# Where the weights lie in a partition: moving the weight buffers below the accumulator and the normalised input in a two-layer recurrent trunk

## The chip, the core and the metric

The kernel runs on one core of one Trainium2 chip. The metric is the device time of one execution in microseconds; the kernel before has a median of 2709.31 us over 3 runs (2709.21 to 2709.97). A profile is one further execution, recorded instruction by instruction.

## What is computed

The reference is a decoder trunk of two layers over 512 positions of 2048 channels, everything in float32:

```
for layer in range(2):
    x = x + mixer(rmsnorm(x) @ w_in) @ w_out
return rmsnorm(x, final_norm)
```

The mixer of layer 0 splits the columns of its projection into an RG-LRU group, an mLSTM group (4 heads) and a gate. The mixer of layer 1 is a Mamba-2 SSD mixer in 8 groups. Nearly all the arithmetic lies in the projections: 128 x 128 blocks of weights against 512 positions.

## The kernel before

**Layout of the work.** Channels lie on the 128 partitions, positions along the free axis. The residual stream `acc` is 16 tiles of [128, 512]. A projection of one column tile is 16 contraction tiles, and a product of two float32 numbers is made of three passes in the type float32r: each weight is split into a rounded part and a rest (`whi`, `wlo`), each moving operand likewise (`xh`/`xl` for the normalised input, `yh`/`yl` and their relatives for what goes into the output projections). The three matmuls are lines 138 to 140:

```
pe.matmul(ps, wh, mh, start=first, stop=False)   # L138
pe.matmul(ps, wh, ml, start=False, stop=False)   # L139
pe.matmul(ps, wl, mh, start=False, stop=last)    # L140
```

"Weights" here is the stationary operand, which a LDWEIGHTS brings into the array ahead of each matmul; the "moving" operand streams past it, 512 columns at a time. So a projection of one column tile is 48 matmuls (a chain), and one group of an output projection is 12 per column tile.

**What is a weight and what moves.** Input projections (tiles `xm`, `zm`, `xl`, `zl` of layer 0, `dt`, `xbc`, `z` of layer 1) move `xh` and `xl`. Output projections (`po`) move `yh`/`yl`, `ylh`/`yll`, `ymh`/`yml`; the head's projections `v`, `o`, `qk` move `xmh`/`xml` or `xch`/`xcl`; one head's `po` moves `xh`/`xl`, which then hold its y. In the last stage the weights of the last output projection are held in `xh` and `xl` themselves. A few matmuls use `ones_r` as weights (`rs`, sums over partitions), and the attention's `num` uses `vh`/`vl` as weights and `Ph`/`Pl` as the moving operand.

**Loads.** `load_w` (line 116) issues one DMA of 512 KB into `wraw`, and per 512 columns ScalarE writes `whi` (line 131) and VectorE writes `wlo` (line 132), at a high priority. There are two `wraw`, four `whi` and four `wlo`, in rotation. The tile framework orders instructions by priority and inserts the waits.

**Staged work.** Everything else of the mixers (convolutions, gates, scans, attention) is in generators that go on after a number of weight chunks, so that TensorE always has a chain to run. Softplus of the LRU's decay, `nlam` (lines 339 and 340, with the helpers at lines 185 to 202), is done once, at the start, on VectorE in three small tiles `ln`.

**Memory.** SBUF pools are stacked: a pool opened later lies above those opened earlier, and a tile lies behind the one allocated before it in its pool, rounded up to 32 bytes. The program's first tile, `prm`, begins at byte 16,512 of each partition and has 3,488 bytes. Adding up the sizes gives the places before: `acc` from byte 22,624; `xh` 55,392 to 88,159; `xl` 88,160 to 120,927; `wraw` 125,088; `whi` 133,280 to 141,471; `wlo` 141,472 to 149,663; above that the pools of each layer, `y` of layer 0 from 182,752 and of layer 1 from 204,512.

Of the kernel before, what the change touches and what calls it, by code (L numbers as in the profile page):

```python
# [9 lines left out]
F32 = mybir.dt.float32  # L10
# [6 lines left out]
P = 128  # L17
# [6 lines left out]

# columns of the packed per-partition parameter array
_W = [
# [12 lines left out]
NPAR = _o  # L39
# how many weight chunks pass before each stage of the mixers' work  # L40
LAG = dict(P=6, rs=2, late=3, dtr=15, CB=5, xtr=6, st=4, yo=1, att_rs=4, vtr=2, aitr=12, num=7, pr=2)
# where the column tiles of the previous group's output projection go in
VB = (2, 2)
# [4 lines left out]
def trunk(ctx, tc, x_t, par, w_in0, w_qkvo, w_lru, w_if, w_out0, w_in1, w_out1, out):  # L48
# [4 lines left out]
    cst = ctx.enter_context(tc.tile_pool(name="cst", bufs=1))  # L53
    wp = ctx.enter_context(tc.tile_pool(name="wp", bufs=1))
    pmm = ctx.enter_context(tc.tile_pool(name="pmm", bufs=3, space=PSUM))
# [16 lines left out]
    v.memset(eps, EPS)  # L72
    warm = cst.tile([P, 1], F32, name="warm")
    sc.activation(warm, eps, AF.Square)
    ones_r = cst.tile([P, P], F32R, name="ones_r")
    ones = ones_r.bitcast(F32)
    r_bc = cst.tile([P, S], F32, name="r_bc")
    acc_t = cst.tile([P, KD, S], F32, name="acc")
    acc = [acc_t[:, k] for k in range(KD)]
    xh = [cst.tile([P, S], F32R, name=f"xh{k}") for k in range(KD)]  # L80
    xl = [cst.tile([P, S], F32R, name=f"xl{k}") for k in range(KD)]
    xpairs = list(zip(xh, xl))
    raws = [cst.tile([P, S + 3], F32, name=f"raw{i}") for i in range(2)]
    for t in raws:
# [6 lines left out]

# [1 line left out]
    gens = []  # L93
# [20 lines left out]

# [1 line left out]
    def load_w(src, dsts=(None, None), pieces=1, ahead=3000):  # L116
# [24 lines left out]

    # one chunk: four contraction tiles, from the k-th on, of n
    def chunk(ps, w, mov, k, n):
# [22 lines left out]

    # in pieces: a reciprocal is slow, and the weights' splits go in between
    def recip(dst, src, w=S):
        for o in range(0, w, P):
            v.reciprocal(dst[:, o:o + P], src[:, o:o + P])  # L170

    # dst = 1 / sqrt(ssq / n + eps) on all partitions; ssq: per-partition partial sums
    def rstd(dst, ssq, n):
# [9 lines left out]

    # log1p(e) for 0 <= e <= 1 as 2 atanh(e / (2 + e))
    def log1p(dst, e, t1, t2):
        v.tensor_scalar(t1, e, 2.0, None, op0=ADD)
        v.reciprocal(t1, t1)
        v.tensor_tensor(t1, e, t1, op=MUL)
        v.tensor_tensor(t2, t1, t1, op=MUL)
        v.tensor_scalar(dst, t2, 1.0 / 15, 1.0 / 13, op0=MUL, op1=ADD)  # L190
        for c in (11, 9, 7, 5, 3, 1):
            v.tensor_tensor(dst, dst, t2, op=MUL)
            v.tensor_scalar(dst, dst, 1.0 / c, None, op0=ADD)
        v.scalar_tensor_tensor(dst, t1, 2.0, dst, op0=MUL, op1=MUL)

    # softplus(s * x) for s = +-1
    def softplus(dst, x, s, t0, t1, t2):
        v.scalar_tensor_tensor(t0, x, -1.0, x, op0=MUL, op1=MAX)
        sc.activation(t0, t0, AF.Exp, scale=-1.0)
        log1p(dst, t0, t1, t2)  # L200
        v.tensor_scalar(t0, x, s, 0.0, op0=MUL, op1=MAX)
        v.tensor_tensor(dst, dst, t0, op=ADD)

    # out of PSUM, ahead of other work: the tensor engine needs the bank
    def evac(o, a, b, op):
        with tc.high_priority(offset=1000):
            v.tensor_tensor(o, a, b, op=op)  # L207

    # causal convolution of a padded tile (bias included)
    def conv(dst, raw, w, b):  # L210
# [3 lines left out]

    # the two parts of acc * norm
    def prenorm(k, norm):
# [9 lines left out]

    # acc += w_out[rows of group g].T @ y, some column tiles
    def outproj(w_out, g, ys, js, done=None):
# [9 lines left out]

    # ================= layer 0 =================
    qd = [dr.tile([2, P, S], F32, name=f"qd{h}") for h in range(NH)]  # L240
# [10 lines left out]

    nlam = L0.tile([P, 16], F32, name="nlam")
    aiT = L0.tile([P, 16], F32, name="aiT")
    ln = [L0.tile([P, 16], F32, name=f"ln{i}") for i in range(3)]

# [29 lines left out]

# [1 line left out]
    pA = tc.tile_pool(name="A", bufs=1)  # L287
# [6 lines left out]

    # four contraction tiles at a time, in the four column strips of the array
    def gate_mm(kt, rhs):
# [4 lines left out]

    # the first two column tiles go along with the loads of x
    ps01 = [mmt("xm"), mmt("xm")]
# [6 lines left out]
    for h in range(NH):  # L310
        xm, xc = [], []
        for t in range(4):
            j = 4 * h + t
            if j > 1:
                ps = mmt("xm")
                proj(ps, w_in0[16 + j], xpairs)
            else:
                ps = ps01[j]
            if j == 0:
                v.tensor_tensor(ssq0[0], ssq0[0], ssq0[1], op=ADD)  # L320
                spawn(rstd(r_bc, ssq0[0], D))
                drain()
            raw = next_raw()
            evac(raw[:, 3:], ps, r_bc, MUL)
            m = xslot("xm")
            split(m[0], m[1], raw[:, 3:])
            xm.append(m)
            a = st("ca")
            conv(a, raw, pc("cm_w", 4 * j, 4), pc("cm_b", j))
            s = st("cs")  # L330
            sc.activation(s, a, AF.Sigmoid)
            v.tensor_tensor(a, a, s, op=MUL)
            c = xslot("xc")
            split(c[0], c[1], a)
            xc.append(c)
            tick()
            if j == 0:
                # -8 softplus(-lam)
                softplus(nlam, pc("lam", 0, 16), -1.0, *ln)
                v.tensor_scalar(nlam, nlam, -8.0, None, op0=MUL)  # L340
# [64 lines left out]

    # gates of all heads: ai = i - G, M = max(0, cummax ai), exp(-m) = exp(-(G + M))
    ready = []

    def gates():
        g_s = st("gs")  # L410
        sc.copy(g_s, ps_g)
        yield 1
        pg = axt("pg")
        pe.matmul(pg[0:36], pc("gsel", 0, 36), g_s, start=True, stop=True)
        g_i, g_f, g_t0, g_t1, g_t2 = [st(f"g{i}")[0:4] for i in range(5)]
        g_G = st("gG")[0:4]
        v.tensor_scalar(g_i, pg[0:4], pc("b_i")[0:4], None, op0=ADD)
        sc.copy(g_f, pg[32:36])
        v.tensor_scalar(g_f, g_f, pc("b_f")[0:4], None, op0=ADD)
        softplus(g_G, g_f, -1.0, g_t0, g_t1, g_t2)  # L420
        for c in range(4):
            cs = slice(c * P, (c + 1) * P)
            v.tensor_tensor_scan(g_t0[:, cs], ones[0:4], g_G[:, cs],
                                 0.0 if c == 0 else g_t0[:, c * P - 1:c * P], op0=MUL, op1=ADD)
        # g_t0 = -G
        v.tensor_tensor(g_i, g_i, g_t0, op=ADD)
        v.tensor_tensor_scan(g_t1, g_i, g_i, 0.0, op0=MAX, op1=MAX)
        v.tensor_tensor(g_t2, g_t0, g_t1, op=SUB)
        sc.activation(g_t2, g_t2, AF.Exp)
        dma(md[0:NH], g_t1)  # L430
        dma(md[NH:2 * NH], g_t2)
        ready.append(True)
        yield LAG["aitr"]
        pt = axt("aitr")
        for s in range(4):
            pe.transpose(pt[:, 4 * s:4 * s + 4], g_i[:, s * P:(s + 1) * P], ident[0:4, 0:4])
        sc.copy(aiT, pt[:, 0:16])
        ready.append(True)

# [1 line left out]
    def lru_tile(j, out_y):  # L441
# [46 lines left out]

# [1 line left out]
    def attention(h, yl, out_y):  # L490
# [115 lines left out]

    # ================= layer 1 =================
    dad = dr.tile([64, S], F32, name="dad")
    ed = dr.tile([64, S], F32, name="ed")
    dcd = dr.tile([64, 2], F32, name="dcd")  # L610

# [1 line left out]
    ps = mmt("dt")  # L613
# [12 lines left out]
    dcb = lt("dcb", shape=(P, 64, 2))  # L626
    na = lt("na", shape=(P, 1))[0:64]
    dc = lt("dc", shape=(P, 2))[0:64]

# [29 lines left out]

    # input projection, convolution and silu of one channel tile of x | B | C  # L660
    def xbc(j, dst):
# [27 lines left out]
    def pair(G, t, xs):  # L689
# [33 lines left out]
        yield LAG["st"]  # L723
        # states at the chunk boundaries
        pst = axt("st")
# [5 lines left out]
        for c in (1, 2):  # L731
# [3 lines left out]
            v.tensor_tensor(Sx[:, c], Sx[:, c], pst[:, c * P:(c + 1) * P], op=ADD)  # L735
        # within the chunks
        pd = axt("yd")
# [5 lines left out]
        yield LAG["yo"]  # L743
        # from the states
        po = axt("yo")
# [75 lines left out]

# [1 line left out]
    wl = []  # L823
# [39 lines left out]

# column tiles, contraction chunks of 8 tiles, each [128, 8 * 128] and contiguous
def _wpack(w):
# [4 lines left out]

# pairs of column tiles, contraction chunks of 4 tiles
def _wpair(w):
# [73 lines left out]
```

## Time and profile before

| what | value |
|---|---|
| median of 3 runs | 2709.31 us |
| profiled execution, span | 2708.4 us |
| TensorE matmul busy | 2680.3 us, 12462 instructions |
| VectorE busy | 1729.7 us |
| ScalarE busy | 1191.2 us |
| GpSimd busy | 118.5 us |
| granted TensorE clock, mean | 0.997 |
| DMA | 297.74 MB, 34.1% of 16 engines' span |

How to read it: "busy" is the union of an engine's recorded intervals. Matmuls are pipelined, so that one is recorded as longer than the distance to the next: the distance from start to start (called the pace below) is what counts, and it is read from the timeline, whose first two columns are the start and the duration in us. In the groups by line, `out<-in` names first what is written, then the moving operand, then the weights.

### The profile page before, as it was taken

The page shows a single profiled execution, that of the slowest core. Times are in us where ns is not written, and L with a number is a line of the kernel's source. Part 1 is how long each engine was busy: PE and PEld are TensorE (multiplying, and loading weights), DVE is VectorE, ACT ScalarE, POOL GpSimd, SP SyncE. Part 2 cuts the span into 40 slices and gives each one's busy share as a digit, 9 for nine tenths or more (in the row PEclk, how much of TensorE's full clock was granted, in tenths as well). Part 3 has the DMA queues.
Part 4 walks back from the last instruction along what each step waited for, and adds up shares of the span by engine and source line. Part 5 has one row for each costly group of instructions (what it writes and reads, how often), then busy time and mean ns, then how long its engine had stood idle before and what let it go on. Part 6 is the DMA issues. An engine that isn't in the chain of part 4 may idle for free.

```text
span 2708.4 us, 33237 instructions
## 1 busy us (share of the span) xinstructions
PE 2680.3 (99%) x12462; PEld 2176.9 (80%) x12462; DVE 1729.7 (64%) x2940; ACT 1191.2 (44%) x1882; POOL 118.5 (4%) x116
## 2 busy tenths in 40 slices
PE   8999999999999999999999999999999999999997
PEld 6778778777888888888888888888888888888887
DVE  8453535387757657665786667656677566675666
ACT  6343333356436436453555343443434434344445
POOL 1000000000000000000200000000000000000004
PEclk9999999999999999999999999999999999999999
DMA  4334342433333333323243332323324233242332
GB/s 164 115 112 135 98 139 90 157 100 122 114 107 105 114 103 107 103 90 99 96 126 109 109 109 94 124 94 109 109 89 130 94 106 111 87 125 95 107 98 101
DMA packets 114385, 297.74 MB, mean 110 GB/s; under 512 B 11688, under 2 KB 34472, under 8 KB 114224
## 3 DMA queue, kind: packets, MB, share of 16 engines
q1 hardware_dynamic: 114224, 295.62, 34.1%
q8 instruction: 98, 1.61, 0.2%
q14 instruction: 63, 0.52, 0.1%
HBM read 278.52 MB, written 17.06 MB: 109 GB/s over the span
## 4 chain that ended last, share of the span: by engine, by line
PE 96%; DVE 3%; DMA 1%; issue 0%; ACT 0%; POOL 0%; SPq 0%; DVEq 0%; ACTq 0%; POOLq 0%
PE po L140 8%; PE po L139 8%; PE po L138 8%; PE xbc L138 7%; PE xbc L140 7%; PE xbc L139 7%; PE z L138 4%; PE z L139 4%; PE z L140 4%; PE xl L138 2%; PE xm L138 2%; PE xm L140 2%; PE xl L139 2%; PE zm L140 2%; PE zm L139 2%; PE xl L140 2%
## 5 line engine op out<-in xcount | busy, mean ns | idle before, releaser
L131 ACT CAST whi<-wraw 128x512 fp32r<-128x512 f32 x886 | 545.7, 616 | 1211.6 <-PE po L139 255.4
L132 DVE TENSOR_TENSOR wlo<-wraw,whi 128x512 fp32r<-128x512 f32 x886 | 609.9, 689 | 467.1 <-ACT whi L131 434.0
L138 PE MATMUL xbc<-xh,whi 128*128 128x512 f32 x768 | 306.8, 399 | 0.0
L139 PE MATMUL xbc<-xl,whi 128*128 128x512 f32 x768 | 303.6, 395 | 0.0
L140 PE MATMUL xbc<-xh,wlo 128*128 128x512 f32 x768 | 303.6, 395 | 0.0
L207 DVE TENSOR_TENSOR acc<-acc,po 128x512 f32<-128x512 f32 (+1 forms) x272 | 176.5, 651 | 172.4 <-PE po L140 171.8
L138 PE MATMUL z<-xh,whi 128*128 128x512 f32 x512 | 205.0, 400 | 0.0
L139 PE MATMUL z<-xl,whi 128*128 128x512 f32 x512 | 202.4, 395 | 0.0
L140 PE MATMUL z<-xh,wlo 128*128 128x512 f32 x512 | 202.3, 395 | 0.0
L138 PE MATMUL po<-yh,whi 128*128 128x512 f32 (+1 forms) x456 | 179.8, 394 | 0.0
L140 PE MATMUL po<-yh,wlo 128*128 128x512 f32 (+1 forms) x456 | 178.6, 392 | 0.0
L139 PE MATMUL po<-yl,whi 128*128 128x512 f32 (+1 forms) x456 | 177.5, 389 | 0.0
L140 PEld LDWEIGHTS xbc<-xh,wlo 128*128 128x128 f32 x768 | 144.4, 188 | 34.9
L138 PEld LDWEIGHTS xbc<-xh,whi 128*128 128x128 f32 x768 | 144.4, 188 | 34.4 <-issue 1.2
L139 PEld LDWEIGHTS xbc<-xl,whi 128*128 128x128 f32 x768 | 144.5, 188 | 33.2
L225 POOL TENSOR_TENSOR ssq<-ssq,sq 128x512 f32<-128x512 f32 (+1 forms) x79 | 89.2, 1129 | 1685.7 <-ACT sq L224 1684.9
L140 PEld LDWEIGHTS z<-xh,wlo 128*128 128x128 f32 x512 | 96.3, 188 | 23.3
L138 PEld LDWEIGHTS z<-xh,whi 128*128 128x128 f32 x512 | 96.3, 188 | 22.0 <-issue 0.2
L139 PEld LDWEIGHTS z<-xl,whi 128*128 128x128 f32 x512 | 96.4, 188 | 21.9
L138 PE MATMUL xm<-xh,whi 128*128 128x512 f32 x256 | 104.1, 407 | 6.5 <-ACT whi L131 5.9
L140 PE MATMUL xm<-xh,wlo 128*128 128x512 f32 x256 | 103.2, 404 | 3.0 <-DVE wlo L132 3.0
L139 PE MATMUL xm<-xl,whi 128*128 128x512 f32 x256 | 103.7, 405 | 0.0
(339 smaller groups left out, 5425.9 us busy)
## 6 DMA issues: line engine op xcount, KB each, us to landing
wraw<-in_w_in_dram SPq DMA_DIRECT2D x288, 512.0 KB, 3.3
wraw<-in_w_out_dram SPq DMA_DIRECT2D x128, 512.0 KB, 3.3
dab<-dad SPq DMA_DIRECT2D x64, 256.0 KB, 3.6
wraw<-in_w_qkvo_dram SPq DMA_DIRECT2D x24, 512.0 KB, 3.3
E<-ed SPq DMA_DIRECT2D x64, 128.0 KB, 3.2
vd<-vn SPq DMA_DIRECT2D x16, 256.0 KB, 3.5
od<-zm SPq DMA_DIRECT2D x16, 256.0 KB, 3.3
V<-vd SPq DMA_DIRECT2D x16, 256.0 KB, 3.8
```

The source lines that it names most:

```text
L131: sc.copy(hi[:, :m], raw[:, i:i + m])
L132: v.tensor_tensor(lo[:, :m], raw[:, i:i + m], hi[:, :m].bitcast(F32), op=SUB)
L138: pe.matmul(ps, wh, mh, start=first, stop=False)
L139: pe.matmul(ps, wh, ml, start=False, stop=False)
L140: pe.matmul(ps, wl, mh, start=False, stop=last)
L207: v.tensor_tensor(o, a, b, op=op)
L225: eng.tensor_tensor(ssq, ssq, sq, op=ADD)
```

## The change

The pools are re-arranged so that the weight buffers are opened right behind a few small tiles. The diff, cut to its core (removed comments are left out):

```diff
-    wp = ctx.enter_context(tc.tile_pool(name="wp", bufs=1))
...
-    warm = cst.tile([P, 1], F32, name="warm")
-    sc.activation(warm, eps, AF.Square)
-    ones_r = cst.tile([P, P], F32R, name="ones_r")
+    nlam = cst.tile([P, 16], F32, name="nlam")
+    aiT = cst.tile([P, 16], F32, name="aiT")
+    sc.activation(nlam[:, 0:1], eps, AF.Square)
+    na = cst.tile([P, 1], F32, name="na")[0:64]
+    dc = cst.tile([P, 2], F32, name="dc")[0:64]
+    wp = ctx.enter_context(tc.tile_pool(name="wp", bufs=1))
+    cst3 = ctx.enter_context(tc.tile_pool(name="cst3", bufs=1))
+    r_bc = cst3.tile([P, S], F32, name="r_bc")
+    acc_t = cst3.tile([P, KD, S], F32, name="acc")
+    acc = [acc_t[:, k] for k in range(KD)]
+    xh = [cst3.tile([P, S], F32R, name=f"xh{k}") for k in range(KD)]
+    xl = [cst3.tile([P, S], F32R, name=f"xl{k}") for k in range(KD)]
+    xpairs = list(zip(xh, xl))
+    cst2 = ctx.enter_context(tc.tile_pool(name="cst2", bufs=1))
+    ones_r = cst2.tile([P, P], F32R, name="ones_r")
     ones = ones_r.bitcast(F32)
-    r_bc = cst.tile([P, S], F32, name="r_bc")
-    acc_t = cst.tile([P, KD, S], F32, name="acc")
-    acc = [acc_t[:, k] for k in range(KD)]
-    xh = [cst.tile([P, S], F32R, name=f"xh{k}") for k in range(KD)]
-    xl = [cst.tile([P, S], F32R, name=f"xl{k}") for k in range(KD)]
-    xpairs = list(zip(xh, xl))
-    raws = [cst.tile([P, S + 3], F32, name=f"raw{i}") for i in range(2)]
+    raws = [cst2.tile([P, S + 3], F32, name=f"raw{i}") for i in range(2)]
...
-    nlam = L0.tile([P, 16], F32, name="nlam")
-    aiT = L0.tile([P, 16], F32, name="aiT")
-    ln = [L0.tile([P, 16], F32, name=f"ln{i}") for i in range(3)]
...
-                softplus(nlam, pc("lam", 0, 16), -1.0, *ln)
+                softplus(nlam, pc("lam", 0, 16), -1.0, *[st("ln")[:, :16] for _ in range(3)])
...
-    na = lt("na", shape=(P, 1))[0:64]
-    dc = lt("dc", shape=(P, 2))[0:64]
```

Adding up sizes as above gives the places after. "mod 256" is the byte within a 256-byte stretch; every slice of an operand that a full-width matmul reads begins at a multiple of 512 bytes from its tile, so one figure holds for the buffer.

| buffer | before, from byte | mod 256 | after, from byte | mod 256 |
|---|---|---|---|---|
| `wraw` | 125,088 | 160 | 20,224 | 0 |
| `whi`, `wlo` | 133,280 and 141,472 | 160 | 28,416 and 36,608 | 0 |
| `acc` | 22,624 | 96 | 46,848 | 0 |
| `xh`, `xl` | 55,392 and 88,160 | 96 | 79,616 and 112,384 | 0 |
| `ones_r` | 20,064 | 96 | 145,152 | 0 |
| `y` of layer 0 | 182,752 | 224 | 182,592 | 64 |
| `y` of layer 1 | 204,512 | 224 | 204,608 | 64 |
| the other tiles of the layers' pools that matmuls read | above 149,983 | 224 | above 149,823 | 64 |

So before, the weights lie above x and below y; after, they lie below both. The tile `warm` is gone (the first activation, which it took, writes a column of `nlam`), and the three `ln` tiles of the softplus come out of the ring of six [128, 512] tiles `s` that the other temporaries of layer 0 use.

## The prediction

> **What bounds the kernel now.** The page comes first: its shares, the clock, and the chain that ended last.
>
> ```profile
> span 2708.4 us, 33237 instructions
> ...
> PE 2680.3 (99%) x12462; PEld 2176.9 (80%) x12462; DVE 1729.7 (64%) x2940; ACT 1191.2 (44%) x1882; POOL 118.5 (4%) x116
> ...
> PEclk9999999999999999999999999999999999999999
> ...
> PE 96%; DVE 3%; DMA 1%; issue 0%; ACT 0%; POOL 0%; SPq 0%; DVEq 0%; ACTq 0%; POOLq 0%
> ...
> L131 ACT CAST whi<-wraw 128x512 fp32r<-128x512 f32 x886 | 545.7, 616 | 1211.6 <-PE po L139 255.4
> L132 DVE TENSOR_TENSOR wlo<-wraw,whi 128x512 fp32r<-128x512 f32 x886 | 609.9, 689 | 467.1 <-ACT whi L131 434.0
> ```
>
> TensorE is never at rest for more than 28 of 2708 us, its clock is full, and 96% of the last chain is matmuls. The feeders wait for TensorE, not it for them: ScalarE sits idle 1211.6 us before `whi`, mostly until a matmul gives a weight buffer back. So no wait is left that a move of buffers could take away. What the change can move is only how fast one matmul follows another. "99% busy" doesn't settle that, because the records of neighbouring matmuls overlap. So I read the pace from the timeline of TensorE, start to start, inside chains that run without a break. First a chain that moves x, then one that moves xc (which lies at the high end, like y):
>
> ```profile
> 1480.43 0.40 PE L138 MATMUL xbc<-xh,whi 128*128 128x512 f32 x1
> ...
> 1489.30 0.39 PE L140 MATMUL xbc<-xh,wlo 128*128 128x512 f32 x1
> ```
>
> ```profile
> 132.41 0.39 PE L138 MATMUL qk<-xch,whi 128*128 128x512 f32 x1
> ...
> 143.17 0.39 PE L140 MATMUL qk<-xch,wlo 128*128 128x512 f32 x1
> ```
>
> Between the quoted rows of the first are 38 steps: 8.87 us / 38 = 233.4 ns. Between those of the second are 47: 10.76 / 47 = 228.9 ns. Same shape, same clock, same helper, same weight buffers; what differs is the moving operand's tile, and so its place: x below the weights on byte 96 of 256, xc above them on byte 224. This difference of 4.5 ns is the only thing in the profile that the change can reach on the path, and all of my forecast hangs on what causes it.
>
> **How many steps are in each class.** From the groups by line, shapes kept apart:
>
> ```profile
> L138 PE MATMUL xbc<-xh,whi 128*128 128x512 f32 x768 | 306.8, 399 | 0.0
> L138 PE MATMUL z<-xh,whi 128*128 128x512 f32 x512 | 205.0, 400 | 0.0
> L138 PE MATMUL xm<-xh,whi 128*128 128x512 f32 x256 | 104.1, 407 | 6.5 <-ACT whi L131 5.9 <-ACT xh L217 0.6
> L138 PE MATMUL zl<-xh,whi 128*128 128x512 f32 x256 | 103.0, 403 | 0.0
> L138 PE MATMUL xl<-xh,whi 128*128 128x512 f32 x256 | 101.4, 396 | 0.0
> L138 PE MATMUL zm<-xh,whi 128*128 128x512 f32 x256 | 101.2, 396 | 0.0
> L138 PE MATMUL po<-xh,whi 128*128 128x512 f32 x64 | 25.3, 395 | 0.0
> L138 PE MATMUL dt<-xh,whi 128*128 128x512 f32 x16 | 6.3, 395 | 0.0
> ```
>
> ```profile
> L138 PE MATMUL po<-yh,whi 128*128 128x512 f32 x448 | 177.5, 396 | 0.0
> L138 PE MATMUL po<-ylh,whi 128*128 128x512 f32 x256 | 101.0, 395 | 0.0
> L138 PE MATMUL po<-ymh,whi 128*128 128x512 f32 x192 | 74.5, 388 | 0.0
> L138 PE MATMUL o<-xmh,whi 128*128 128x512 f32 x64 | 26.3, 411 | 0.0
> L138 PE MATMUL v<-xmh,whi 128*128 128x512 f32 x64 | 25.7, 402 | 0.0
> L138 PE MATMUL qk<-xch,whi 128*128 128x512 f32 x64 | 25.2, 394 | 0.0
> ```
>
> Each row is one of three passes. x: (768 + 512 + 4 x 256 + 64 + 16) x 3 = 7152 steps. High end: (448 + 256 + 192 + 3 x 64) x 3 = 3264 steps.
>
> **The main term.** I take it that what makes x slow is that the weights lie above it: with the weights below, a step that moves x costs what a step that moves y costs. This gives 7152 x 4.5 ns = 32.2 us. Not every chain at the high end is fast, though. This one moves y out of the same buffers as its neighbours:
>
> ```profile
> 1749.19 0.40 PE L139 MATMUL po<-yl,whi 128*128 128x512 f32 x1
> ...
> 1754.33 0.40 PE L140 MATMUL po<-yh,wlo 128*128 128x512 f32 x1
> ```
>
> 22 steps in 5.14 us are 233.6 ns. It starts after a stall of TensorE, and there are few such chains. I deduct 5% for x chains that would do the same (1.6 us), and 0.5 us for the 119 matmuls of the first 45 us, which wait for loads:
>
> ```profile
> 0.00:45.00 45.00, 34.95 (x119) 25.69 (x120) 35.43 (x65) 29.71 (x51) 11.39 (x11) 0.92 0.57 200
> 45.00:526.00 481.00, 481.00 (x2126) 381.77 (x2124) 223.25 (x332) 185.48 (x312) 0.00 (x0) 1.00 0.37 117
> ```
>
> The gain is 30 us. The high-end steps keep their pace: the distance from weights to y changes from 64 to 64 within 256 bytes, and the weights stay below.
>
> Can the feeders keep up? One `whi` and one `wlo` serve 12 steps, 12 x 0.229 = 2.75 us; in that time ScalarE needs 0.616 us for the one and VectorE 0.689 us for the other (the means of the rows L131 and L132). A span shorter by 1% raises VectorE's share from 64% to 65%. So no feeder becomes the bound.
>
> **The small parts.** The softplus for `nlam` changes its buffers:
>
> ```profile
> L198 DVE SCALAR_TENSOR_TENSOR ln<-prm x1: 1261/1261/1261, 35.0 to 35.0; 128x16 f32<-128x16 f32 x1
> ...
> L202 DVE TENSOR_TENSOR nlam<-nlam,ln x1: 174/174/174, 43.8 to 43.8; 128x16 f32<-128x16 f32 x1
> ```
>
> It now takes three of the ring's six slots, behind `ca` and `cs` of the first column tile, so I expect it later, after 50 us, among that tile's convolution. It is some 20 operations of 0.17 us, about 4 us of VectorE. Queued behind them are the next evacuations and `wlo`; both are issued at a higher priority and so wait for one operation of 0.17 us at most. The cover is the slack of TensorE's queue in that stretch: it is busy 481.00 of 481.00 us from 45 us on. I cost it at nothing; without the cover it is 4 us, and if the quiet first 45 us get shorter because VectorE is free there, it is a gain of 1 to 2 us. `na`, `dc` and `warm` move or vanish without an instruction more; `ones_r` is weights for 28 steps in all (`rs`), nothing. The stage of 256 columns at the end, where x holds weights, I leave at its time; its pace depends on place too:
>
> ```profile
> 2691.92 0.28 PE L138 MATMUL po<-yh,whi 128*128 128x256 f32 x1
> ...
> 2692.51 0.28 PE L140 MATMUL po<-yh,wlo 128*128 128x256 f32 x1
> 2692.63 0.28 PE L138 MATMUL po<-xh,whi 128*128 128x256 f32 x1
> ...
> 2693.20 0.28 PE L140 MATMUL po<-xh,wlo 128*128 128x256 f32 x1
> ```
>
> 5 steps in 0.59 us are 118 ns with y, 5 in 0.57 are 114 with x. Some 380 such steps at 4 ns either way are 1.5 us, for the range.
>
> The sum: 2708.4 - 30 = 2678.4 us for the span; the median of the runs lies 0.9 us above this span, so 2679.3 us. The bounds of this case are 2672 (both deductions fall away, the softplus and the end stage gain) to 2690 (a third of the x chains stay slow, the softplus costs 4 us).
>
> A rule that speaks against it stands in the Trainium skill, page "SBUF — State Buffer", section "Who interferes with whom": TensorE reads its moving operand and its weights through two independent ports and never waits on anyone. By that rule the place of the weights can't matter, and the sum would be 2709. The two chains above, 233.4 against 228.9 ns, do not agree with a pace that no place can change; they don't say which property of the place does it.
>
> **Rival 1: nothing happens (2709 us, 2704 to 2714).** Before, three things differ at once between x and y: the order against the weights, the byte within 256 (96 against 224), and the distance to the weights within 256 (192 against 64). After, x gets the good order but a distance of 0. The nearest row with distance 0 is the attention's `num`, where weights and moving operand are both on byte 224:
>
> ```profile
> 691.14 0.40 PE L138 MATMUL num<-Ph,vh 128*128 128x512 f32 x1
> 691.38 0.39 PE L139 MATMUL num<-Pl,vh 128*128 128x512 f32 x1
> 691.60 0.40 PE L140 MATMUL num<-Ph,vl 128*128 128x512 f32 x1
> 691.84 0.34 PE L138 MATMUL num<-Ph,vh 128*128 128x384 f32 x1
> ```
>
> Three steps in 0.70 us, 233.3 ns: the slow pace. If distance is the cause, x stays there. Against: in `num` the weights also lie above, so order explains it as well. The slow y chain speaks for this rival too, since it shows that place alone doesn't settle the pace, and so does the end stage, where x over weights above it is the faster one. Its price is the lost 30 us, less at most the 1.5 us and 4 us of the small parts.
>
> **Rival 2: slower, because y loses its pace (2723 us).** If the cause is the byte within 256 at which the moving operand starts, 224 is the only place that is known to be fast, and the change takes all high-end tiles from 224 to 64 while x goes from 96 to 0, neither of which the trace shows. Then x stays at 233.4 and y joins it: 3264 x 4.5 ns = 14.7 us, less the few that are slow already, +14: 2723 us. It decides where the steady high-end chains pass 230 ns: with x unchanged, one ns there is 3.3 us. For it: `num` has 224 and is slow, so 224 is at least no guarantee, which leaves room for what the other operand's byte does. Against: x/y differ in order all the way through, and the slices of y begin on bytes of one kind in both layers.
>
> **Rival 3: much faster (2632 us).** All operands on multiples of 64 bytes, which no matmul's operands in the trace before are (96, 160 and 224 leave 32), could cut both paces below 228.9. One more step of the same size, 4.5 ns on all 10,416 steps, is 47 us beyond the forecast. No row shows it. The Trainium skill, page "TensorE: Matmul & The Clock Gate", section "Back-to-back issue gap", gives about 216 ns for 512 columns at full clock as the gap of a single matmul stream; by that figure an estimate would be 7152 x 17.4 + 3264 x 12.9 ns = 167 us, 2543 us. No chain of the trace runs at it.
>
> **How the numbers follow.** Order as the cause (forecast): 0.47, since it is the one account that agrees with x, y and `num` together. Rival 1: 0.27, for the slow y chain and the distance. Rival 2: 0.18. Rival 3: 0.08. The range leaves rival 3 out and holds the others with their bounds: 2672 to 2725; the likeliest case alone has 2672 to 2690. About 0.2%, 5.4 us, is what a measurement of this kernel can tell from no change. Faster is the forecast and rival 3: 0.55; same 0.26, nearly all of rival 1; slower 0.19, rival 2 and a small rest.
>
> **What would show it.** Right: in chains of `xbc` and `z` the starts are 229 ns apart instead of 233.4, the mean durations of the x groups fall by some 4 ns (L138 `xbc` from 399), chains of `qk` and `po` stay near 229, and TensorE's busy time falls by about 30 us while the idle 28 us stay. Wrong: x chains at 233 (rival 1), y chains at 233 (rival 2), any chain clearly under 228 (rival 3), or a gap on TensorE between 45 and 70 us that the later softplus makes.

## The result, and the profile after

The kernel before took 2709.26 us (median of 4 runs, 2708.61 to 2709.97), the changed one 2667.77 us (4 runs, 2667.15 to 2669.20). The ratio is 0.9846 with a 95% interval of 0.9834 to 0.9858: 41.5 us faster. The forecast was 2679.3 us, with 2672 as the low end of its range. The sign was right, the gain is larger than forecast, and, as the experiments show, the cause was not the one that I gave; that the sign came out was luck.

First the page of the changed kernel: span, busy time of the engines, the chain that ended last, and the two feeders. The line numbers moved: L131 and L132 are now L137 and L138, the three matmul lines L138 to L140 are L144 to L146.

```profile
span 2665.7 us, 33237 instructions
...
PE 2636.7 (99%) x12462; PEld 2172.9 (82%) x12462; DVE 1728.0 (65%) x2940; ACT 1194.1 (45%) x1884; POOL 118.4 (4%) x116
...
PE 95%; DVE 2%; DMA 0%; issue 0%; ACT 0%; POOL 0%; DVEq 0%; ACTq 0%; POOLq 0%
...
L137 ACT CAST whi<-wraw 128x512 fp32r<-128x512 f32 x886 | 545.3, 616 | 1166.1 <-PE po L145 259.9
L138 DVE TENSOR_TENSOR wlo<-wraw,whi 128x512 fp32r<-128x512 f32 x886 | 610.4, 690 | 437.8 <-ACT whi L137 414.0
```

The picture is the one of before with less of it: the same 12462 matmuls, 43.6 us less busy time on TensorE (2680.3 to 2636.7), 29.0 us of idle time against 28.1. The feeders' own times are unchanged (616 and 690 ns); only their idle time shrank. So nearly the whole gain is pace. The timeline of TensorE in the changed kernel shows whose, first in a chain that moves x:

```profile
1455.16 0.39 PE L144 MATMUL xbc<-xh,whi 128*128 128x512 f32 x1
...
1465.13 0.39 PE L146 MATMUL xbc<-xh,wlo 128*128 128x512 f32 x1
```

and in one that moves xc, at the high end:

```profile
131.62 0.39 PE L146 MATMUL qk<-xch,wlo 128*128 128x512 f32 x1
...
139.86 0.39 PE L146 MATMUL qk<-xch,wlo 128*128 128x512 f32 x1
```

In the first are 44 steps in 9.97 us, 226.6 ns; before it was 233.4. In the second 36 steps in 8.24 us, 228.9 ns, as before. x did not come down to y's pace: it went past it. To compare kernels I use from here on the mean of all start-to-start steps of a class between neighbouring records of 512 columns with weights from `whi` or `wlo`, some 6,900 for x and some 3,200 for the high end, without those over 15 ns above the class's median (stalls and missing records). It is 233.26 ns for x before and 227.26 after, 229.19 and 229.29 for the high end. Such a mean is good to some 0.1 ns: it shifts by less with how the borders of a class are drawn.

That gives the account of the gain: 7152 x 6.0 ns = 42.9 us from x, less 0.3 us that the high end lost, and the rest is small. The view by windows shows how much more work a stretch holds:

```profile
0.00:45.00 45.00, 33.95 (x126) 24.68 (x127) 33.94 (x47) 30.43 (x52) 11.87 (x11) 0.96 0.56 200
45.00:526.00 481.00, 481.00 (x2163) 388.00 (x2162) 228.63 (x359) 193.29 (x323) 0.00 (x0) 1.00 0.37 123
```

2163 matmuls in the 481 us in which there were 2126, at the same full clock. The groups by line, shapes kept apart, hold a warning for the reader:

```profile
L144 PE MATMUL xbc<-xh,whi 128*128 128x512 f32 x768 | 302.3, 394 | 0.0
L144 PE MATMUL z<-xh,whi 128*128 128x512 f32 x512 | 202.3, 395 | 0.0
L144 PE MATMUL po<-yh,whi 128*128 128x512 f32 x448 | 178.8, 399 | 0.0
```

The mean of `xbc` falls from 399 to 394 and that of `z` from 400 to 395, by some 5 ns where the pace fell by 6. But `po` rises from 396 to 399 while the steps of its class stay at 229 ns. One record's length is not the distance to the next record; the pace has to be read start to start.

### The profile page after: what moved, and what is told of

It is laid out like the page before. It is cut to its first block, busy times and chain, and to the rows that moved or that the text cites. A ratio compares the mean times of both kernels' runs of the same rounds, so it can differ in the third digit from the quotient of the medians.

```text
span 2665.7 us, 33237 instructions
## 1 busy us (share of the span) xinstructions
PE 2636.7 (99%) x12462; PEld 2172.9 (82%) x12462; DVE 1728.0 (65%) x2940; ACT 1194.1 (45%) x1884; POOL 118.4 (4%) x116
## 4 chain that ended last, share of the span: by engine, by line
PE 95%; DVE 2%; DMA 0%; issue 0%; ACT 0%; POOL 0%; DVEq 0%; ACTq 0%; POOLq 0%
PE po L144 8%; PE po L146 8%; PE po L145 8%; PE xbc L144 7%; PE xbc L146 7%; PE xbc L145 7%; PE z L144 4%; PE z L146 4%; PE z L145 4%; PE xl L144 2%; PE xl L145 2%; PE xl L146 2%; PE zm L145 2%; PE zm L146 2%; PE zm L144 2%; PE zl L144 2%
## 5 line engine op out<-in xcount | busy, mean ns | idle before, releaser
L137 ACT CAST whi<-wraw 128x512 fp32r<-128x512 f32 x886 | 545.3, 616 | 1166.1 <-PE po L145 259.9
L138 DVE TENSOR_TENSOR wlo<-wraw,whi 128x512 fp32r<-128x512 f32 x886 | 610.4, 690 | 437.8 <-ACT whi L137 414.0
L144 PE MATMUL xbc<-xh,whi 128*128 128x512 f32 x768 | 302.3, 394 | 0.0
L146 PE MATMUL xbc<-xh,wlo 128*128 128x512 f32 x768 | 299.2, 390 | 0.0
L144 PE MATMUL z<-xh,whi 128*128 128x512 f32 x512 | 202.3, 395 | 0.0
L146 PE MATMUL z<-xh,wlo 128*128 128x512 f32 x512 | 199.7, 390 | 0.0
L144 PE MATMUL po<-yh,whi 128*128 128x512 f32 (+1 forms) x456 | 181.1, 397 | 0.0
L146 PE MATMUL po<-yh,wlo 128*128 128x512 f32 (+1 forms) x456 | 177.9, 390 | 0.0
L146 PEld LDWEIGHTS xbc<-xh,wlo 128*128 128x128 f32 x768 | 144.1, 188 | 30.4
L144 PEld LDWEIGHTS xbc<-xh,whi 128*128 128x128 f32 x768 | 144.2, 188 | 30.1 <-issue 1.2
L146 PEld LDWEIGHTS z<-xh,wlo 128*128 128x128 f32 x512 | 96.1, 188 | 20.7
L144 PEld LDWEIGHTS z<-xh,whi 128*128 128x128 f32 x512 | 96.2, 188 | 19.3 <-issue 0.2
L144 PE MATMUL xm<-xh,whi 128*128 128x512 f32 x256 | 101.5, 396 | 6.2 <-ACT whi L137 5.9
L146 PE MATMUL xm<-xh,wlo 128*128 128x512 f32 x256 | 100.8, 395 | 2.9 <-DVE wlo L138 2.9
```

What stands on the lines that cost most here:

```text
L137: sc.copy(hi[:, :m], raw[:, i:i + m])
L138: v.tensor_tensor(lo[:, :m], raw[:, i:i + m], hi[:, :m].bitcast(F32), op=SUB)
```

## The experiments

The theory of the forecast was **order**: x is slow because the weights lie above it. The rivals that were still open after the result were **alignment** (everything on multiples of 64 or 256 bytes) and **distance** (the bytes from the weights to the moving operand, modulo 256: for x 192 before and 0 after, for y 64 both times).

**Order put back.** The changed kernel with the weight buffers above x again; all operands keep their byte modulo 256.

```diff
-    wp = ctx.enter_context(tc.tile_pool(name="wp", bufs=1))
     cst3 = ctx.enter_context(tc.tile_pool(name="cst3", bufs=1))
...
     xpairs = list(zip(xh, xl))
+    wp = ctx.enter_context(tc.tile_pool(name="wp", bufs=1))
     cst2 = ctx.enter_context(tc.tile_pool(name="cst2", bufs=1))
```

> The changed kernel with one line moved: the weight buffers are opened behind x instead of ahead of it, so they lie above x (bytes 120,576 to 145,151; x from 55,040 to 120,575), everything still on byte 0 of 256, y still on byte 64. Order as the cause (my theory): x goes back to 233 ns a step, about 2709 us. Place within 256 bytes as the cause (rival): x keeps the 227 ns of the changed kernel and the time stays within 3 us of 2668 us.

Measured: 2667.59 us, ratio 0.9846 (0.9830 to 0.9863). The timeline of this kernel:

```profile
1454.97 0.39 PE L146 MATMUL xbc<-xh,wlo 128*128 128x512 f32 x1
...
1465.86 0.39 PE L146 MATMUL xbc<-xh,wlo 128*128 128x512 f32 x1
```

48 steps in 10.89 us, 226.9 ns, with the weights above x as they were before the change. My theory falls: the order is worth nothing.

**Alignment taken away.** Everything behind `dc` shifted by 32 bytes, so that weights and x begin on byte 32 of 256 and y on 96; all distances stay.

```diff
-    dc = cst.tile([P, 2], F32, name="dc")[0:64]
+    dc = cst.tile([P, 16], F32, name="dc")[0:64, 0:2]
```

> The changed kernel with 32 bytes more ahead of the weights: weights and x on byte 32 of 256, y on byte 96, order and distances kept. Order or distance as the cause: x at 227 ns, 2668 us within 3. The operands' own alignment (multiples of 64 or 256 bytes) as the cause: x between 229 and 233 ns, 2682 to 2710 us.

Measured: 2667.16 us, ratio 0.9844 (0.9830 to 0.9859). The timeline of this kernel:

```profile
1454.66 0.39 PE L144 MATMUL xbc<-xh,whi 128*128 128x512 f32 x1
...
1464.63 0.39 PE L146 MATMUL xbc<-xh,wlo 128*128 128x512 f32 x1
```

44 steps in 9.97 us, 226.6 ns; the means of the classes are 227.20 ns for x and 229.32 for y. The multiples of 256 (and of 64) in the change's description do nothing by themselves.

**Distance changed, order and multiples of 64 kept.** Padding of 64 bytes ahead of x moves x to a distance of 64 and y to 128.

```diff
-    r_bc = cst3.tile([P, S], F32, name="r_bc")
+    r_bc = cst3.tile([P, S + 16], F32, name="r_bc")[:, :S]
```

> The changed kernel with 64 bytes more between the weights and acc: weights on byte 0 of 256, x on 64, y on 128, order kept. Order as the cause: x stays at 227 ns, 2668 us. Distance between moving operand and weights within 256 bytes as the cause: x takes the pace that y has at distance 64, 229 ns, so 7152 x 2 = 14 us more, 2682 us, and y at distance 128 shows a pace not seen yet.

Measured: 2690.80 us, ratio 0.9931 (0.9917 to 0.9946), 23.0 us above the changed kernel. x's timeline:

```profile
1456.97 0.40 PE L144 MATMUL xbc<-xh,whi 128*128 128x512 f32 x1
...
1465.91 0.39 PE L144 MATMUL xbc<-xh,whi 128*128 128x512 f32 x1
```

39 steps in 8.94 us, 229.2 ns: at y's distance x takes y's pace. And y, now at 128, slows to a mean of 232.40. The two terms, 7152 x 1.86 = 13.3 us and 3264 x 3.11 = 10.2 us, add up to 23.5 us, against 23.0 measured.

**The pace by itself.** A kernel of nothing but chains of 96 matmuls of 512 columns, for each place of weights and moving operand, with the weights below (`lo`) and above (`hi`) and, once the tile is filled, no other engine at work. All of it ran in one execution. The two letters of a name are the bytes modulo 256 of weights and moving operand, a to h for 0, 32, ... 224.

```python
for o, wb in (("lo", WL), ("hi", WH)):
    for wi, xi in cfg:
...
        last = chain(f"{o}{L[wi]}{L[xi]}", wb + 32 * wi, X + 32 * xi, 2)
```

> Leaves out the whole computation: only chains of 96 matmuls (the three passes over 16 weight slices and 32 moving tiles) over one large tile, with no loads and no other engine beside them, at 16 pairs of bytes within 256 for weights and moving operand, each with the weights below and above the moving operand, and all of it twice. Order as the cause: the 16 chains with the weights below run at 227 to 229 ns and the 16 with the weights above at 233. Distance as the cause: the pace depends on the pair and not on the order; equal bytes give 227, moving 64 above gives 229, moving 192 above (weights 160, moving 96) gives 233. Traffic of the other engines as a part of the cause: all 32 run at one pace.

From its timeline, the first and the last matmul of some chains, 95 steps apart:

```profile
728.13 0.39 PE L74 MATMUL loaa<-big 128*128 128x512 f32 x1
...
749.71 0.39 PE L76 MATMUL loaa<-big 128*128 128x512 f32 x1
...
772.34 0.40 PE L74 MATMUL loac<-big 128*128 128x512 f32 x1
...
794.09 0.39 PE L76 MATMUL loac<-big 128*128 128x512 f32 x1
...
839.13 0.40 PE L74 MATMUL loaf<-big 128*128 128x512 f32 x1
...
861.38 0.39 PE L76 MATMUL loaf<-big 128*128 128x512 f32 x1
...
1081.51 0.39 PE L74 MATMUL hiaa<-big 128*128 128x512 f32 x1
...
1103.08 0.39 PE L76 MATMUL hiaa<-big 128*128 128x512 f32 x1
...
1259.77 0.40 PE L74 MATMUL hifd<-big 128*128 128x512 f32 x1
...
1281.94 0.39 PE L76 MATMUL hifd<-big 128*128 128x512 f32 x1
```

That is 227.2 ns at distance 0, 228.9 at 64, 234.2 at 160; 227.1 at 0 with the weights above; and 233.4 for `hifd`, weights on 160 and x on 96, which is the place that x had before the change. The first steps of a chain are irregular; over the last 48 steps, from the same records:

| distance modulo 256 | chains | ns per step |
|---|---|---|
| 0 | aa, bb, cc, dd, ee, ff, hh | 226.67 |
| 64 | ac, fh | 228.9 |
| 32, 96, 128, 192, 224 | ab, ad, ae, ag, fd, ah | 233.33 |
| 160 | af | 234.33 |

`lo` and `hi` agree, as do both repeats, within 0.05 ns. So the distance alone sets the pace in these chains: not the order, not the byte itself, and no other engine's traffic, of which there is none here.

**y at distance 0 as well.** What this points to: the changed kernel still has y at 64. Two small tiles are merged and y is padded, so that weights, x and y all begin on byte 224 of 256, a multiple of 32 only.

```diff
-    eps = cst.tile([P, 1], F32, name="eps")
+    en = cst.tile([P, 2], F32, name="en")
+    eps, na = en[:, 0:1], en[0:64, 1:2]
...
-    na = cst.tile([P, 1], F32, name="na")[0:64]
...
-    raws = [cst2.tile([P, S + 3], F32, name=f"raw{i}") for i in range(2)]
+    raws = [cst2.tile([P, S + 3 + 48 * i], F32, name=f"raw{i}")[:, :S + 3] for i in range(2)]
```

> The changed kernel with eps and na in one tile (32 bytes fewer ahead of the weights) and 192 bytes of padding behind x: weights, x and y all lie on byte 224 of 256, so that both x and y have the distance 0 to the weights; before, y had 64. Distance theory: x stays at the changed kernel's pace (227 ns on average), and y's 3264 steps go from 229.3 to x's 227.3 ns: 6.5 us less, 2661 us (2659 to 2663). Rival (multiples of 64 or 256 bytes matter as well, beside the distance): x and y lose them, 2668 or more. Rival (y is held at 229 by something else, such as the reuse of its slots or the stalls ahead of its short chains): y doesn't move, 2667.8 us.

Measured: 2659.99 us (5 runs, 2659.22 to 2662.41), ratio to before 0.9817 (0.9803 to 0.9830), the fastest version. Its timeline in the chain of `qk`:

```profile
131.25 0.39 PE L144 MATMUL qk<-xch,whi 128*128 128x512 f32 x1
...
141.91 0.39 PE L146 MATMUL qk<-xch,wlo 128*128 128x512 f32 x1
```

47 steps in 10.66 us, 226.8 ns; the mean of the class falls from 229.29 to 227.29, 3264 x 2.0 = 6.5 us of the 7.8 us against the changed kernel.

**A bad distance in the changed order.** 128 bytes of padding ahead of x: x at 128, y at 192, the weights below both, all on multiples of 64.

```diff
-    r_bc = cst3.tile([P, S], F32, name="r_bc")
+    r_bc = cst3.tile([P, S + 32], F32, name="r_bc")[:, :S]
```

> The changed kernel with 128 bytes of padding ahead of x: weights on byte 0, x on 128, y on 192 of 256; the order (weights below both) and multiples of 64 bytes stay as the change made them. Distance theory, with the paces that the chains without other work showed: x at 233.3 (+6.0 ns x 7152 = 43 us), y at distance 192 at 233.3 (+4.0 ns x 3264 = 13 us): 2724 us, slower than the kernel before, although the order is the changed one. Order theory: 2668 us, or at most 2679.

Measured: 2718.43 us, ratio 1.0032 (1.0020 to 1.0044): slower than before, although the weights lie below x and y, as the change put them. Its timeline, x and then xc:

```profile
1454.64 0.40 PE L144 MATMUL z<-xh,whi 128*128 128x512 f32 x1
...
1459.99 0.39 PE L146 MATMUL z<-xh,wlo 128*128 128x512 f32 x1
```

```profile
132.70 0.40 PE L144 MATMUL qk<-xch,whi 128*128 128x512 f32 x1
...
142.97 0.40 PE L146 MATMUL qk<-xch,wlo 128*128 128x512 f32 x1
```

x: 23 steps in 5.35 us, 232.6 ns; xc: 44 steps in 10.27 us, 233.4. It came out 5.6 us below the 2724 expected, since x at 128 has a mean of 232.56 and not the 233.33 of the bare chains: 7152 x 0.77 = 5.5 us. The run with y at 128 showed the same (232.40). Why 128 is a little quicker inside the kernel stays open.

**The softplus alone.** The kernel before, with the softplus's three tiles taken from the ring. In the first run the three tiles of 64 bytes go, and with them the pools of layer 0 slide by 192 bytes; in the second they stay allocated and unused.

```diff
-    ln = [L0.tile([P, 16], F32, name=f"ln{i}") for i in range(3)]
...
-                softplus(nlam, pc("lam", 0, 16), -1.0, *ln)
+                softplus(nlam, pc("lam", 0, 16), -1.0, *[st("ln")[:, :16] for _ in range(3)])
```

> The kernel before with one part of the change alone: the softplus takes three slots of the ring, and its own three small tiles of 64 bytes go. This frees 192 bytes ahead of y, so y slides from byte 224 to 32 and its distance to the weights goes from 64 to 128; weights and x stay where they were. Distance theory: x as before, y 229.2 to about 232.4 to 233.3 ns: 3264 x 3.2 to 4.1 = 10 to 13 us more, 2720 to 2723 us. Softplus theory (its place in time decides, the address doesn't): 2709 us, within 2 us, or up to 4 us more if it stands in the way of the evacuations.

> As the run before, but the three small tiles stay allocated, unused, so that y, x and weights all keep the addresses that they had before the change: the softplus's new place in the order of work alone. Distance theory: no change, 2709 us within 1.5 us. Rival (part of the 41.5 us, or of a loss, comes from the softplus): 2705 or less, or 2713 or more.

Measured: 2709.67 us, ratio 0.9999 (0.9991 to 1.0008) with the addresses kept: the softplus's new place in the order of work costs nothing. With the tiles gone 2715.64 us, ratio 1.0022 (1.0014 to 1.0031): dropping 192 bytes that no matmul touches makes the kernel slower. The timeline of that run:

```profile
132.68 0.40 PE L138 MATMUL qk<-xch,whi 128*128 128x512 f32 x1
...
143.65 0.39 PE L140 MATMUL qk<-xch,wlo 128*128 128x512 f32 x1
```

47 steps in 10.97 us, 233.4 ns, where the same chain had 228.9. I had expected 10 to 13 us, on all 3264 steps of the high end; but only layer 0's tiles slid, and layer 1's y stayed where it was. The moved rows are those of `ylh`, `ymh`, `xmh` and `xch`: (256 + 192 + 3 x 64) x 3 = 1920 steps, with a mean of 232.60 instead of 229.19: 6.5 us of the measured 6.2.

## Why the prediction was right and where it was wrong

**Right: what bounds the kernel and what the change can reach.** TensorE is still busy 99%, no wait took the place of another (29.0 us idle against 28.1), and the time moved by the number of steps times a change of pace. The count of 7152 steps carries the result: 7152 x 6.0 = 42.9 us of a span that fell by 42.7.

**Wrong: the step "I take it that what makes x slow is that the weights lie above it".** With the weights above x the time is 2667.59 us, the same as below. With the weights below x and x at a distance of 128 it is 2718.43 us, more than before the change, so the forecast got its sign only because the new places happened to bring x to a distance of 0. The cause is the distance to the weights modulo 256, which the prediction had named as the property behind rival 1, and then priced the wrong way round.

**Where it went wrong: the row of `num`.** Rival 1 said that at distance 0 x would stay at 233 ns, because three steps of `num` at distance 0 took 233.3 ns. This row was taken for the pace that distance 0 gives. The same group in the kernel where y lies at distance 0 as well, with `num`'s own operands still at distance 0 and on byte 224, shows that it was not:

```profile
685.88 0.39 PE L144 MATMUL num<-Ph,vh 128*128 128x512 f32 x1
686.10 0.39 PE L145 MATMUL num<-Pl,vh 128*128 128x512 f32 x1
686.33 0.39 PE L146 MATMUL num<-Ph,vl 128*128 128x512 f32 x1
686.56 0.33 PE L144 MATMUL num<-Ph,vh 128*128 128x384 f32 x1
```

Three steps in 0.68 us, 226.7 ns. All 16 groups of `num` run there at 225 to 228 ns a step; before the change each of the 16 had a step of 231 ns or more. Its own operands have the same byte and the same distance in both; what differs is above all the distance of the chains before and after it. That these set its pace is inferred and wasn't tested, but the row can't be the pace of distance 0. The bare chains show it too. These are the first four starts and the last of a chain at distance 0 (weights and moving operand both on byte 64), the slowest start of the seven chains at distance 0 with the weights below:

```profile
1016.09 0.40 PE L74 MATMUL locc<-big 128*128 128x512 f32 x1
1016.33 0.40 PE L75 MATMUL locc<-big 128*128 128x512 f32 x1
1016.56 0.40 PE L76 MATMUL locc<-big 128*128 128x512 f32 x1
1016.80 0.39 PE L74 MATMUL locc<-big 128*128 128x512 f32 x1
...
1037.67 0.39 PE L76 MATMUL locc<-big 128*128 128x512 f32 x1
```

The first three steps take 0.71 us, some 235 ns each; the 92 behind them 20.87 us, 226.8 ns each. Three steps don't show the pace to which a long chain settles. Had the row been left out, distance 0 would have been a place that no row shows, and rival 1's condition could have ended on either side; the x chains at 192 and the y chains at 64 were evidence for distance just as much as for order.

**Wrong by this: the size.** The term was 7152 x 4.5 ns with y's pace of 229 as the floor; x reached 227.26, so the term measured 6.0 ns each, 42.9 instead of 32.2 us. The prediction had written that any chain clearly under 228 would prove it wrong; the x chains are such.

**The two deductions.** 1.6 us for x chains that would stay slow: no x chain of ten steps or more in the trace after has a mean above 232 ns. 0.5 us for the first 45 us: there TensorE's busy time fell by 1.0 us instead (34.95 to 33.95), with 126 matmuls in place of 119. Without the deductions, the forecast would have been 2677.2 us, still 9.4 us too high; the main term is what failed. The ends of the range don't follow from their terms either: without the deductions and with gains of 2 and 1.5 us the low end is 2673.7 us and not 2672, and with a third of the x chains slow and 4 us for the softplus the high end is some 2692 us and not 2690. The measured time lies below all of these.

**The small parts held.** The softplus runs later, as said, from the view of the tile `ln` after the change:

```profile
L204 DVE SCALAR_TENSOR_TENSOR ln<-prm x1: 165/165/165, 52.9 to 52.9; 128x16 f32<-128x16 f32 x1
...
L208 DVE TENSOR_TENSOR nlam<-nlam,ln x1: 176/176/176, 69.3 to 69.3; 128x16 f32<-128x16 f32 x1
```

It starts at 52.9 us where it had started at 35.0 and ends at 69.5, while TensorE is busy without a gap, and alone it is worth nothing (ratio 0.9999). The end stage of 256 columns, allowed 1.5 us either way, lost about 0.5: the mean step of its 384 matmuls goes from 118.1 to 119.3 ns. Its part in which x meets weights of `whi` and `wlo` shows it:

```profile
2648.83 0.29 PE L144 MATMUL po<-xh,whi 128*128 128x256 f32 x1
...
2649.44 0.28 PE L146 MATMUL po<-xh,wlo 128*128 128x256 f32 x1
```

5 steps in 0.61 us, 122 ns, against 114 before. At 256 columns distance 0 is not the fast place.

**The rivals.** Rival 2, the byte of the moving operand: out, since y kept 229 ns on byte 64 (and on 96), and x has 227 on bytes 0, 32 and 224. Its picture, x and y both slow, does exist; the distances 128 and 192 make it (2718.43 us). Rival 3, alignment to 64 bytes: out, since the pace stays at byte 32 and byte 224; but its sign, a pace below 228.9, is what came. (Its premise had a slip: by the sizes, the matrices in `prm`, from byte 16,576, did lie on multiples of 64 before the change; they serve a few small matmuls only.)

**The two rules that the prediction cited.** By the Trainium skill, page "SBUF — State Buffer", section "Who interferes with whom", TensorE reads its moving operand and its weights through independent ports; the prediction drew from it that the place can't matter, 2709 us. The bare chains do not agree with this reading: with no other engine at work, the place of the weights relative to the moving operand moves the step from 226.67 to 234.33 ns. What in the hardware ties the two together was not measured. The Trainium skill, page "TensorE: Matmul & The Clock Gate", section "Back-to-back issue gap", gives about 216 ns for 512 columns at the full clock, and calls it the gap of an isolated matmul, not of a stream as the prediction has it. No run reached it; the shortest steady step in any run is 226.67 ns.

One thing stays open. At distance 64 a few chains run at 233.3 ns throughout: 4 of the high end before, 1 after, and none at distance 0. The slow y chain of the prediction is one of them, and it followed a stall. But a stall isn't needed: in the run with x at 64, six `xbc` chains do the same right behind short matmuls that ran without a break. The first of them:

```profile
1508.77 0.40 PE L145 MATMUL xbc<-xl,whi 128*128 128x512 f32 x1
...
1516.70 0.40 PE L146 MATMUL xbc<-xh,wlo 128*128 128x512 f32 x1
```

34 steps in 7.93 us, 233.2 ns, where most chains of that class take 229. So the distance 64 has two steady paces in the kernel, and what chooses between them wasn't tried.

## What to carry to other kernels

Where TensorE is busy all the time and nothing waits, read the pace start to start and by operand: two classes of the same shape at different paces are a gain that neither busy shares nor waits show. In the long float32r chains of 512 columns here, the best of the eight distances tried (multiples of 32 bytes) is 0: weights and moving operand begin on the same byte modulo 256, whichever lies lower. Any small tile added or dropped ahead of them can move them off it. To judge a place from a trace, take long chains and leave out their start (in the chain on byte 64 above, the first 23 steps still have a mean of 228.7 ns), and when several properties of a place change at once, price each for itself before choosing one.

## What the runs showed of the hardware that I had not expected

In the bare chains, a step of 512 columns with a weight load each has four steady paces, by the distance modulo 256 alone: 226.67 ns at 0, 228.9 at 64, 233.33 at 32, 96, 128, 192 and 224, and 234.33 at 160. In this kernel the whole span from best to worst layout tried is 2659.99 to 2718.43 us, 2.2%, with the same 12462 matmuls. At 256 columns the ranking is another: x against `whi`, 16 steps in each run, takes 114.9 to 117.1 ns at 192 (three runs), 117.7 at 64, 118.6 at 128 and 119.4 to 120.0 at 0 (four runs). Distance 0 is the slowest of these four; 192 and 64 are hardly told apart, since the runs at 192 alone spread by 2 ns.
